# One hybrid decoder trunk on one core: the order in which the three mixers' pieces are traced

## The chip, the core and the metric

The kernel runs on 1 core of one Trainium2 chip. The time is microseconds of device time for one execution, from the first to the last instruction and what the launch adds around them. The engines are named as in the profile: PE (matmul) with PEld (its weight loads), DVE (vector), ACT (scalar), POOL, and SP, which here only issues DMAs.

## The reference

Two layers over 256 tokens of width 1024, batch 1, all float32. Each layer does:

```
h      = RMSNorm(x) * (1 + scale) + shift            # scale, shift, gate from silu(c) @ ada_w
cols   = h @ w_in                                    # 1024 x 9544
y_rw   = RWKV-7(cols)   # 8 heads of 64, delta-rule state, needs an inverse of a triangular matrix per 128 tokens
y_ssd  = Mamba-2 SSD(cols)  # conv of width 4, 4 groups x 4 heads, chunks of 128
y_fox  = FoX attention(cols)  # 8 heads of 64, causal, forget-gate bias
merged = sum_b sigmoid(gate_b) * (y_b @ proj_b)
x      = x + gate * (merged @ w_out)
x      = x + gate_f * FFN(h')    # layer 0: dense SwiGLU 2816; layer 1: top-2 of 8 experts of 3584
```

## The kernel before

Activations lie transposed in SBUF: features on 128 partitions, the 256 tokens in the free dimension. Every large product is done in three matmuls (`mm3`, line 124): a float32 weight is split into a high part (ACT, line 156) and a rest (DVE, line 157), and high x high, high x rest and rest x high are summed in PSUM. One **projection step** is 128 output columns over K = 1024: 24 matmuls of 256 columns, and two pairs of splits of 128x512. `stationary` (377) does two steps in one PSUM bank of tag `pd`; `project_rows` (391) does 256 columns into a `pd` and a `ps` bank; `project_cols` (386) loads the weight and calls `stationary`.

**The mixers of a layer** are Python generators. `rwkv_half` (487), called for two halves of 4 heads, r0 and r1, has the projections of k, r, v; then elementwise work on DVE and ACT, the pair matrices (line 612), a block inverse in six doubling levels (lines 649 to 674, with 32x32 transposes on DVE at 654), the state products (693 to 731) and the group norm (736 to 746). `ssd_group` (789), s0 to s3, has four projection steps with the convolution (799 to 805), the chunk products, and two gate projection steps (869). `fox_half` (898), f0 and f1, has three `project_rows` whose banks ACT copies out at line 906, then attention for four heads. `gates` (967) projects one branch's gate for all of `merged`; `merge` (976) multiplies one branch's y by its projection, for the other two branches with their gates, and adds.

**The order written out** is `ORDER` (51): a list for each layer of names, walked by lines 1376 to 1405. Each name runs its generator to its next `yield`, and there are few of these: r0 and r1 have four pieces (projections; all up to the pair matrices; all levels; state products, then the end), an s group three, an f half three, a merge one for each quarter. `mo` and `md` take the next half part of the modulation vectors of later sub-layers: 2 MB of `ada_w` are loaded (line 210; `mo`: four loads of 512 KB into two buffers `araw`; `md`: eight of 256 KB into buffers `u`), and eight operations of 128x512 on DVE (223, 225) sum them. The first merge is that of RWKV in the list before (`m0`), with its gates in `G`.

The instructions are not run in the order traced: line 1493 asks the framework to lay out each engine's queue by its own timing estimate, in which the trace order is the preference between those that are ready. The projections among themselves keep the trace order, as their weight loads do on SP's queue. What the pieces share: 3 weight buffers `raw` of 1 MB, 5 pairs `hi`/`lo`, 15 buffers `u` (all of RWKV's and FoX's values and the sums of `mo`), 4 buffers `b8` (y of RWKV and FoX, pair matrices, `merged`), 2 PSUM banks `pd`, 4 `pm`, 2 `ps`.

Of the kernel before, what the change touches and what calls it, by code (L numbers as in the profile page):

```python
# [63 lines left out]
def trunk(  # L64
# [312 lines left out]
    def stationary(raw, n, evac):  # L377

        ps = dbank()
        for q in range(0, n, P):  # L380
            m = min(P, n - q)
            o = ps[:m, q * 2:q * 2 + T]
            accumulate(o, raw[:, :, q:q + m], (hh, hl))
            evac(q // P, o)

    def project_cols(wsrc, c0, n, evac):
        for p0 in range(0, n, 256):
            w = min(256, n - p0)
            stationary(load_raw(rows(wsrc, 0, D, c0 + p0, w), KD, w), w, lambda i, ps: evac(p0 // P + i, ps))

    def project_rows(wsrc, c0, y):
# [3 lines left out]
        for kg in range(4):  # L395
            hi, lo = split_part(raw[:, 2 * kg:2 * kg + 2, :])
            for t in range(2):
                tb = slice(t * P, (t + 1) * P)
                for k in range(2):
                    kt = 2 * kg + k  # L400
                    mm3(ps[t], (y[0][:, kt, tb], y[1][:, kt, tb]), (hi[:, k, :], lo[:, k, :]), kt == 0, kt == KD - 1)
        return ps
# [33 lines left out]
    def stages(f):  # L436

        def start(*a):
            g = f(*a)
            return lambda: next(g, None)  # L440
        return start
# [17 lines left out]
    def rwkv(mx, l, prm, lora):  # L459
# [10 lines left out]
        project_cols(w_in[l], 1536, 288, lambda i, ps: shift(wa if i == 0 else gl[:ps.shape[0], i - 1, :], ps, 12 + i))  # L470
# [14 lines left out]
        return [y[:, 0], y[:, 1]], lambda jp: stages(rwkv_half)(mx, l, prm, lora, jp, shift, wa, gl, vd, vup, y)  # L485

    def rwkv_half(mx, l, prm, lora, jp, shift, wa, gl, vd, vup, y):
# [8 lines left out]
        for dst, g in ((k, 1), (r, 0), (v, 2)):  # L496
            project_cols(w_in[l], g * RW + jp * 256, 256, lambda i, ps: shift(dst[:, i, :], ps, 4 * g + 2 * jp + i))
# [14 lines left out]
        for jj in J:  # L512
            js = slice((2 * jp + jj) * P, (2 * jp + jj + 1) * P)
            for dst, hb, base in ((s, 0, W0), (th, 1, A0)):
                ps = mbank()[:, :T]
                mm(ps, wau[hblock(hb), js], wa[hblock(hb), :])
                act.activation(dst[:, jj, :], ps, AF.Tanh, scale=0.5, bias=col(pph, base, jj))
        dve.tensor_scalar_add(s, s, 1.0)
# [16 lines left out]


# [6 lines left out]
        for t in range(2):  # L543
            for jj in J:
                mm(ps[:, t * 4 + 2 * jj:t * 4 + 2 * jj + 2], sq[:, jj, t * P:(t + 1) * P], headsel)
        ss, rs = small(8, "r"), small(8, "r")
# [9 lines left out]


# [17 lines left out]


# [4 lines left out]


# [5 lines left out]
        act.activation(vrow, ps, AF.Copy)  # L588
        ps = mbank().rearrange("p (c f) -> p c f", c=2)
# [3 lines left out]
        act.activation(brow, ps, AF.Copy)  # L593

# [6 lines left out]
        for ch in range(2):  # L601
# [4 lines left out]
            for dst, src in ((mats[:, 0], bt), (mats[:, 1], kt)):  # L606
                for hb in range(2):
                    ps = mbank()
                    hp = hblock(hb)
                    for jj in J:  # L610
# [3 lines left out]
                                        ps.rearrange("p (q m) -> p q m", q=2))  # L614
            mbs.append(mats[:, 0])
            mks.append(mats[:, 1])
        yield
# [23 lines left out]
        for ch in range(2):  # L641
# [6 lines left out]
            act.activation(tls[ch], pz, AF.Copy)  # L648
        for lv in range(1, 6):
            odd = slice(1, 4, 2) if lv == 5 else slice(0, 4)  # L650
            for ch in range(2):
                pz = level(ch, lv, tls[ch])
                for q in range(4):
                    dve.transpose(blk(bds[ch], q)[:, odd, bcol(q)], by4(blk(pz, q))[:, odd, :])  # L654
            for ch in range(2):
# [10 lines left out]
            for ch in range(2):  # L666
# [5 lines left out]
                if lv == 4:  # L672
                    for n in range(4):
                        pool.tensor_copy(blk(tms[ch], n)[:, :, bcol(n)], by4(blk(tls[ch], n)))
        for ch in range(2):
# [4 lines left out]
            act.activation(ums[ch], pz, AF.Copy)  # L680
        h0, h1 = slice(0, 64), slice(64, 128)
# [10 lines left out]
        yield  # L692
        for ch in range(2):
# [10 lines left out]
            for hb in range(2):  # L704
                act.activation(halves(rr, hb), pb[hb][:, 0:2, :], AF.Copy)
            psa = mbank().rearrange("p (q f) -> p q f", f=64)
# [3 lines left out]
            act.activation(sa, psa[:, 0:4, :], AF.Copy)  # L710

# [10 lines left out]
            act.activation(yc, py, AF.Copy)  # L722
            pr = mbank()[:, :256]
# [8 lines left out]


# [13 lines left out]
        yield  # L747
# [750 lines left out]
```

## Time and profile before

| | |
|---|---|
| time, median of 3 runs | 2234.21 us (2226.03 to 2235.48) |
| the profiled execution | 2224.52 us |
| its span, first to last instruction | 2222.8 us |
| PE, PEld, DVE, ACT, POOL busy in it | 2115.0, 1811.2, 1798.8, 1386.1, 152.1 us |
| mean granted TensorE clock | 0.970 |

The page gives busy times; ends of matmuls in it are modelled, so a busy PE is not a PE at its full rate. Stages are read by cutting the span into stretches and asking busy time, number of instructions and granted clock (1.00 is 2.4 GHz, 0.50 is 1.2 GHz) of each. The stretches used: layer 0's first RWKV half from 60 to 182 us, its second half to 306, FoX and the merges to 478; then the output projection, the dense FFN and the next norm to 722; layer 1's RWKV halves from 750 to 876 and to 1026, its FoX and merges to 1168; the output projection and the experts to the end.

### The profile page before, as it was taken

The page shows a single profiled execution, that of the slowest core. Times are in us where ns is not written, and L with a number is a line of the kernel's source. Part 1 is how long each engine was busy: PE and PEld are TensorE (multiplying, and loading weights), DVE is VectorE, ACT ScalarE, POOL GpSimd, SP SyncE. Part 2 cuts the span into 40 slices and gives each one's busy share as a digit, 9 for nine tenths or more (in the row PEclk, how much of TensorE's full clock was granted, in tenths as well). Part 3 has the DMA queues.
Part 4 walks back from the last instruction along what each step waited for, and adds up shares of the span by engine and source line. Part 5 has one row for each costly group of instructions (what it writes and reads, how often), then busy time and mean ns, then how long its engine had stood idle before and what let it go on. Part 6 is the DMA issues. An engine that isn't in the chain of part 4 may idle for free.

```text
span 2222.8 us, 35724 instructions
## 1 busy us (share of the span) xinstructions
PE 2115.0 (95%) x13489; PEld 1811.2 (81%) x13489; DVE 1798.8 (81%) x2822; ACT 1386.1 (62%) x2204; POOL 152.1 (7%) x180
## 2 busy tenths in 40 slices
PE   7899899999998889989998999999999999999998
PEld 4777789998997877868998788888888887888776
DVE  4977776777776797756768999999999989999887
ACT  3454455555454545434555877878878777878775
POOL 2211200000000031211002000000000000000000
PEclk9999999999999998988998999999999999999999
DMA  8423254667884533414556999999999999999994
GB/s 304 128 83 95 77 172 156 213 198 259 294 286 137 145 108 93 138 53 130 184 176 251 337 362 359 324 368 367 374 337 352 355 362 336 342 364 368 336 363 151
DMA packets 316101, 546.68 MB, mean 246 GB/s; under 512 B 11952, under 2 KB 143536, under 8 KB 315920
## 3 DMA queue, kind: packets, MB, share of 16 engines
q1 hardware_dynamic: 315920, 544.31, 71.1%
q8 instruction: 108, 1.77, 0.3%
q14 instruction: 73, 0.60, 0.1%
HBM read 543.22 MB, written 1.05 MB: 245 GB/s over the span
## 4 chain that ended last, share of the span: by engine, by line
PE 79%; DVE 13%; issue 3%; ACT 2%; DMA 2%; POOL 0%; SPq 0%; DVEq 0%; ACTq 0%; POOLq 0%
PE pd L122 37%; PE pm L122 33%; PE ps L122 7%; DVE lo L157 5%; PE pm L131 1%; DVE u L654 1%; DMA araw<-in_ada_w_dram 1%; PE ps L131 1%; ACT hi L156 1%; DMA b<-in_ada_w_dram 1%; DVE cu L802 1%; DVE xr L1257 1%; DVE u L225 0%; DMA raw<-in_moe_w_gu_dram 0%; DVE b L612 0%
## 5 line engine op out<-in xcount | busy, mean ns | idle before, releaser
L156 ACT ACTIVATE hi<-raw 128x1024 fp32r<-128x1024 f32 (+2 forms) x1201 | 1027.7, 870 | 522.4 <-PE pd L122 277.0
L157 DVE TENSOR_TENSOR lo<-raw,hi 128x1024 fp32r<-128x1024 f32 (+2 forms) x1197 | 1154.6, 990 | 211.6 <-ACT hi L156 189.8
L122 PE MATMUL pd<-hh,hi 128*128 128x256 f32 (+2 forms) x1208 | 352.7, 293 | 15.3 <-ACT hh L362 3.9
L122 PE MATMUL pd<-hh,lo 128*128 128x256 f32 (+2 forms) x1208 | 346.5, 287 | 0.0
L122 PE MATMUL pd<-hl,hi 128*128 128x256 f32 (+2 forms) x1208 | 345.7, 286 | 0.3
L122 PE MATMUL pm<-lo,hh 128*128 128x512 f32 x672 | 266.7, 397 | 3.0 <-DVE lo L157 2.8
L122 PE MATMUL pm<-hi,hh 128*128 128x512 f32 x672 | 266.9, 397 | 0.1
L122 PE MATMUL pm<-hi,hl 128*128 128x512 f32 x672 | 263.0, 392 | 0.0
L122 PEld LDWEIGHTS pd<-hh,hi 128*128 128x128 f32 (+2 forms) x1208 | 231.9, 192 | 28.3 <-issue 5.6
L122 PEld LDWEIGHTS pd<-hh,lo 128*128 128x128 f32 (+2 forms) x1208 | 231.5, 192 | 6.1 <-issue 3.9
L122 PEld LDWEIGHTS pd<-hl,hi 128*128 128x128 f32 (+2 forms) x1208 | 232.7, 193 | 4.3 <-issue 2.3
L122 PE MATMUL pd<-lo,hi 128*128 128x512 f32 x448 | 174.7, 390 | 0.0
L122 PE MATMUL pd<-hi,hi 128*128 128x512 f32 x448 | 170.9, 391 | 0.1
L122 PE MATMUL pd<-hi,lo 128*128 128x512 f32 x448 | 167.8, 389 | 0.0
L122 PEld LDWEIGHTS pm<-lo,hh 128*128 128x128 f32 x672 | 126.8, 189 | 32.1 <-DVE lo L157 5.5
L122 PEld LDWEIGHTS pm<-hi,hh 128*128 128x128 f32 x672 | 126.5, 188 | 29.3 <-ACT hi L156 1.4
L122 PEld LDWEIGHTS pm<-hi,hl 128*128 128x128 f32 x672 | 126.7, 189 | 26.5
L122 PE MATMUL pm<-hi,more 128*128 128x512 f32 x448 | 142.1, 392 | 0.0
L122 PEld LDWEIGHTS pd<-hi,hi 128*128 128x128 f32 x448 | 84.1, 188 | 18.4 <-ACT hi L405 0.5
L122 PEld LDWEIGHTS pd<-hi,lo 128*128 128x128 f32 x448 | 84.1, 188 | 17.8
L122 PEld LDWEIGHTS pd<-lo,hi 128*128 128x128 f32 x448 | 84.1, 188 | 17.6
L122 PEld LDWEIGHTS pm<-hi,more 128*128 128x128 f32 x448 | 84.1, 188 | 17.5 <-ACT hi L156 0.3
(423 smaller groups left out, 3467.0 us busy)
## 6 DMA issues: line engine op xcount, KB each, us to landing
raw<-in_moe_w_gu_dram SPq DMA_DIRECT2D x224, 1024.0 KB, 7.0
raw<-in_moe_w_down_dram SPq DMA_DIRECT2D x110, 1024.0 KB, 6.8
raw<-in_w_in_dram SPq DMA_DIRECT2D x66, 1024.0 KB, 5.4
araw<-in_ada_w_dram SPq DMA_DIRECT2D x68, 512.0 KB, 4.3
raw<-in_ffn_w_gu_dram SPq DMA_DIRECT2D x22, 1024.0 KB, 6.8
raw<-in_ffn_w_down_dram SPq DMA_DIRECT2D x11, 1024.0 KB, 6.5
raw<-in_w_in_dram SPq DMA_DIRECT2D x16, 512.0 KB, 5.1
raw<-in_proj_ssd_dram SPq DMA_DIRECT2D x8, 1024.0 KB, 5.2
```

The costliest lines, as they stand in the source:

```text
L122: pe.matmul(o, lhsT, rhs, start=start, stop=stop)
L131: pe.transpose(o, i, ident[:n, :n])
L156: act.activation(hi, raw, AF.Copy)
L157: minus.tensor_sub(lo, raw, hi.bitcast(F32))
L654: dve.transpose(blk(bds[ch], q)[:, odd, bcol(q)], by4(blk(pz, q))[:, odd, :])
L802: dve.scalar_tensor_tensor(cu[:, s:T], ps[:, 0:T - s], pph[:, w:w + 1], cu[:, s:T], op0=ALU.mult, op1=ALU.add)
L1257: dve.tensor_add(xr[:, t, hs], xr[:, t, hs], po)
```

## The change

Every generator gets a `yield` after each projection step and each link of its chain of small operations: an RWKV half now has 45 steps, an s group 14, an f half 21, the gates 9, the first merge 9, the others 17 (`STEPS`). `ORDER` becomes one list of segments for both layers; a segment has one to three streams, and their steps are traced in turn, spread evenly over the segment. "`r1:25`" is 25 steps of r1, "`s2.`" what is left of s2. The gates made ahead are those of SSD (`b` = 1), which is merged first (`ma`), RWKV second (`mb`), FoX third (`mc`). `md` is gone: all six (layer 0) and five (layer 1) half parts of the modulation go by `mo`. What each operation computes is unchanged; `project_out` and `rwkv`'s first projection are still run whole (`whole`).

```diff
-ORDER = [
-    (
-        "rw r0 r0 mo r0 r0 fx sd s0 s0 s0 s1 s1 s1 r1 r1 r1 r0 s2 mo s2 s2 f0 r1 r1 s3 mo G f0 mo G s3 s3 G "
-        "f0 G m0 f1 m0 f1 m0 md md m1 md m0 m1 m1 md f1 md md md m1 m2 gm m2 md m2 m2"
-    ).split(),
-    (
-        "rw r0 r0 mo r0 sd s0 s0 r0 r0 s0 s1 mo s1 s1 s2 r1 r1 G r1 s2 fx r1 G s2 r1 G s3 s3 mo f0 f0 s3 G m0 "
-        "f0 m0 mo m0 m0 f1 md f1 m1 m1 md md md gm m1 md m1 f1 m2 m2 m2 md md md m2"
-    ).split(),
+STEPS = dict(r=45, s=14, f=21, G=9, ma=9, mb=17, mc=17)
+ORDER = 2 * [
+    [
+        ["rw"], ["r0:7"], ["sd"],
+        ["r0:25", "s0. s1:4", "mo"],
+        ["r0:8", "s1. s2:4", "mo"],
+        ["r0.", "r1:7 s2:2", "mo"],
+        ["r1:25", "s2. s3. G:4", "mo"],
+        ["r1:8", "G. ma:4", "mo"],
+        ["r1.", "fx f0:8 ma:2"],
+        ["f0.", "ma. f1:7", "mo mo"],
+        ["f1.", "mb:8", "mo mo"],
+        ["mb.", "mo"], ["gm"], ["mc."],
+    ],
 ]
...
             accumulate(o, raw[:, :, q:q + m], (hh, hl))
             evac(q // P, o)
+            yield
...
-            stationary(load_raw(rows(wsrc, 0, D, c0 + p0, w), KD, w), w, lambda i, ps: evac(p0 // P + i, ps))
+            yield from stationary(load_raw(rows(wsrc, 0, D, c0 + p0, w), KD, w), w, lambda i, ps, i0=p0 // P: evac(i0 + i, ps))
...
+            for segment in ORDER[l]:
+                streams = [steps(stream) for stream in segment]
+                for _, _, name in sorted(((i + 0.5) / len(x), k, name) for k, x in enumerate(streams) for i, name in enumerate(x)):
+                    assert take(name), (name, counts, taken)
```

## Rows read from the trace of the kernel before

**Rows 1.** The page's head: the span, and busy us (share) xinstructions by engine.

```profile
span 2222.8 us, 35724 instructions
...
PE 2115.0 (95%) x13489; PEld 1811.2 (81%) x13489; DVE 1798.8 (81%) x2822; ACT 1386.1 (62%) x2204; POOL 152.1 (7%) x180
```

**Rows 2.** Stretch, length, busy us (x) of PE, PEld, DVE, ACT, POOL; clock; DMA, GB/s.

```profile
60.00:182.00 122.00, 107.28 (x917) 91.94 (x916) 92.72 (x208) 56.48 (x138) 23.51 (x27) 0.92 0.32 95
182.00:306.00 124.00, 113.75 (x976) 95.84 (x974) 93.91 (x214) 60.45 (x139) 29.00 (x32) 0.96 0.38 113
306.00:440.00 134.00, 132.92 (x1128) 124.23 (x1126) 97.96 (x189) 76.17 (x175) 5.41 (x6) 1.00 0.58 185
440.00:478.00 38.00, 38.00 (x318) 36.72 (x317) 25.41 (x48) 21.88 (x40) 0.00 (x0) 1.00 0.58 181
...
750.00:876.00 126.00, 112.81 (x958) 94.58 (x956) 105.59 (x234) 64.85 (x160) 28.89 (x31) 0.94 0.35 101
876.00:1026.00 150.00, 133.64 (x1060) 112.26 (x1061) 104.07 (x223) 65.96 (x149) 27.84 (x31) 0.88 0.33 99
1026.00:1138.00 112.00, 112.00 (x939) 103.82 (x938) 74.85 (x144) 62.89 (x140) 5.18 (x5) 1.00 0.52 167
1138.00:1168.00 30.00, 30.00 (x267) 30.00 (x266) 20.22 (x38) 17.67 (x33) 0.00 (x0) 1.00 0.68 210
```

**Rows 3.** The same view, 1000 to 1010 us.

```profile
1000.00:1010.00 10.00, 9.26 (x35) 5.51 (x35) 1.68 (x6) 0.89 (x3) 1.01 (x1) 0.50 0.00 0
```

**Rows 4.** The same, only instructions on tile lo: PE, PEld, DVE, POOL.

```profile
60.00:182.00 122.00, 42.74 (x144) 29.50 (x144) 25.64 (x36) 0.00 (x0) 0.92 0.32 95
182.00:306.00 124.00, 48.87 (x168) 32.98 (x168) 28.96 (x42) 0.00 (x0) 0.96 0.38 113
306.00:440.00 134.00, 77.85 (x279) 52.33 (x280) 47.86 (x70) 0.00 (x0) 1.00 0.58 185
...
750.00:876.00 126.00, 43.41 (x149) 29.39 (x148) 28.57 (x39) 0.00 (x0) 0.94 0.35 101
876.00:1026.00 150.00, 55.76 (x188) 38.30 (x188) 32.67 (x47) 0.00 (x0) 0.88 0.33 99
1026.00:1138.00 112.00, 65.56 (x235) 43.95 (x236) 39.37 (x58) 0.00 (x0) 1.00 0.52 167
```

**Rows 5.** In order of time: start us, us, instruction [idle before <-releaser]; r1's state products.

```profile
992.11 0.88 PE L122 MATMUL pm<-b,u 128*64 128x128 f32 x12 [0.47 <-ACT u L710]
```

**Rows 6.** As rows 4, on tile lo, in stretches of 10 us.

```profile
240.00:250.00 10.00, 0.00 (x0) 0.00 (x0) 0.00 (x0) 0.00 (x0) 0.86 0.01 2
...
870.00:880.00 10.00, 0.00 (x0) 0.00 (x0) 0.00 (x0) 0.00 (x0) 0.76 0.22 67
...
990.00:1000.00 10.00, 0.17 (x1) 0.00 (x0) 0.69 (x1) 0.00 (x0) 0.90 0.15 51
1000.00:1010.00 10.00, 0.00 (x0) 0.00 (x0) 0.00 (x0) 0.00 (x0) 0.50 0.00 0
```

**Rows 7.** In order of time, ACT, layer 1.

```profile
1011.45 0.56 ACT L758 ACTIVATE u<-pm,pcol 128x256 f32<-128x256 f32 x1 [6.13 <-PE pm L131]
1011.91 0.37 ACT L906 ACTIVATE u<-pd 128x256 f32<-128x256 f32 x1
```

**Rows 8.** In order of time, DVE, layer 0.

```profile
100.10 0.73 DVE L612 COPY_PREDICATED b<-mmask,pm 128x512 f32<-128x512 uint8 x1
...
100.92 0.70 DVE L805 SCALAR_TENSOR_TENSOR xb<-zt,cu 128x256 f32<-128x256 f32 x1
...
106.66 0.68 DVE L157 TENSOR_TENSOR lo<-raw,hi 128x512 fp32r<-128x512 f32 x1
107.26 0.28 DVE L644 TENSOR_TENSOR c<-pm,icomp 128x128 f32<-128x128 f32 x1
```

**Rows 9.** Line 225, 60 to 306 us: xcount, ns min/median/max, first to last start.

```profile
L225 DVE SCALAR_TENSOR_TENSOR u<-araw,silc,u x14: 730/744/1653, 87.6 to 281.6; 128x512 f32<-128x512 f32 x14
```

**Rows 10.** SP's waits, 750 to 1026 us: waited for, us in total, times, longest.

```profile
SPq L210 <- DVE u L225: 63.9, 11, 23.1
```

More of the change, by code (lines that the diff above doesn't have):

```diff
@@ L434, in pair, with whole @@
         return keep(a, [P, KD, T], F32R), keep(b, [P, KD, T], F32R)
[L436 to L441, printed above, removed]
+    def whole(g):
+        while True:
+            try:
+                next(g)
+            except StopIteration as e:
+                return e.value
     def hblock(hb):
@@ L555, in rwkv_half @@
         dve.tensor_mul(kk, kk, ps)
+        yield
         kn = u()
@@ L809, in ssd_group @@
             nc.sync.dma_start(raw[:, :, q * P:(q + 1) * P], rows(w_in[l], 0, D, XBC_OFF + 1024 + 512 * q + g * P, P))
-        stationary(raw, 256, lambda i, ps: conv(2 + i, ps))
-        project_cols(w_in[l], XBC_OFF + g * 256, 256, conv)
-        yield
+        yield from stationary(raw, 256, lambda i, ps: conv(2 + i, ps))
+        yield from project_cols(w_in[l], XBC_OFF + g * 256, 256, conv)
         hc = lambda a, ch, n=4: a[:, ch * 16 + 4 * g:ch * 16 + 4 * g + n]
@@ L1374, in trunk, with part, take @@
             dtr = small_cols(l, mx)
-            run = {}
-            for step in ORDER[l]:
+            run, made, counts = {}, {}, {}
+            done = object()
+            def part(step):
                 i = int(step[1]) if step[1:] in tuple("0123") else 0
-                if step == "rw":
-                    y_rw, rw = rwkv(mx, l, prm, lora)
-                elif step == "sd":
-                    y_ssd, sd = ssd(mx, l, prm, dtr)
-                elif step == "fx":
-                    y_fox, fx = fox(mx, l, prm, dtr)
-                elif step == "mo":
-                    mod_next(mx, 0)
-                elif step == "md":
-                    mod_next(mx, MOD_LEFT[l], True)
-                elif step == "gm":
+                if step == "G":
+                    made["merged"] = mx("b8", [P, KD, T], bufs=NB8)
+                    return gates(mx, l, prm, 1, made["merged"])
+                if step[0] == "m":
+                    b = (1, 0, 2)["abc".index(step[1])]
+                    return merge(mx, l, prm, b, made["merged"], made["y"][b], (proj_rw, proj_ssd, proj_fox)[b][l], (4, 8, 4)[b], b == 1)
+                return made[step[0]](i)
+            def take(token):
+                if token == "rw":
+                    made.setdefault("y", {})[0], made["r"] = rwkv(mx, l, prm, lora)
+                elif token == "sd":
+                    made["y"][1], made["s"] = ssd(mx, l, prm, dtr)
+                elif token == "fx":
+                    made["y"][2], made["f"] = fox(mx, l, prm, dtr)
+                elif token == "mo":
+                    mod_next(mx, MOD_LEFT[l])
+                elif token == "gm":
                     while mod_late and mod_late[0][2] == 2:
@@ L1391, in trunk, with steps @@
                     gm = keep("vfirst", [P, 2, 512]) if l == 1 else mx("u2", [P, 2, 512])
[L1392 to L1405 removed]
+                    made["gm"] = [gm[:, 0], gm[:, 1]]
+                    mod_row(lambda: unit(mx, 4, P), l, 2, 0.5, made["gm"])
+                else:
+                    if token not in run:
+                        run[token] = part(token)
+                    if run[token] is None:
+                        return False
+                    counts[token] = counts.get(token, 0) + 1
+                    if next(run[token], done) is done:
+                        run[token] = None
+                return True
+            taken = {}
+            def steps(stream):
+                names = []
+                for word in stream.split():
+                    name, _, n = word.rstrip(".").partition(":")
+                    n = STEPS[name if name in STEPS else name[0]] - taken.get(name, 0) if word[-1] == "." else int(n or 1)
+                    taken[name] = taken.get(name, 0) + n
+                    names += [name] * n
+                return names
+            for segment in ORDER[l]:
+                streams = [steps(stream) for stream in segment]
+                for _, _, name in sorted(((i + 0.5) / len(x), k, name) for k, x in enumerate(streams) for i, name in enumerate(x)):
+                    assert take(name), (name, counts, taken)
+            assert not any(run.values()), [k for k in run if run[k]]
+            merged, gm = made["merged"], made["gm"]
             dump(f"merged{l}", merged)
```

68 lines of the change are left out of this document (41 added, 27 removed).

## The prediction

> **What bounds the kernel now.** I read the head of the page first: PE is busy 2115.0 of 2222.8 us, every other engine 81% or less [rows 1]. PE sets the pace, and the change adds and removes no matmul: it can win only where PE waits or runs slowly, in the two stretches with mixers, 60 to 478 and 750 to 1168 us. The other 1387 us keep their order.
>
> Next the stages [rows 2]. FoX and the merges (306 to 478, 1026 to 1168) are full: PE 132.92 of 134, 38.00 of 38, 112.00 of 112, 30.00 of 30, the clock at 1.00 (2.4 GHz). The RWKV stages are not: PE 107.28 of 122, 113.75 of 124, 112.81 of 126, 133.64 of 150, the clock at 0.92, 0.96, 0.94, 0.88.
>
> Busy time flatters these stages. From 1000 to 1010 us PE counts as busy for 9.26 us with 35 small matmuls, at clock 0.50 (1.2 GHz) [rows 3]. The Trainium skill ("Perfetto Trace Analysis", Identifying the Most-Contended Engine) says that matmul busy share is a poor measure of headroom and that the share of weight loads is a better one. The row agrees: 5.51 of those 10 us. By PE's busy time the four RWKV stages leave 522 - 467.5 = 54.5 us as the most to be won, by the weight loads 522 - 394.6 = 127 us; the sum below uses neither.
>
> I count instead. Projection matmuls come in threes, one of which reads `lo`. In the pure stretches 440 to 478 and 1138 to 1168 all matmuls are projections: (38 + 30) / (318 + 267) = 0.116 us each [rows 2]. So a stage's projections take 3 x its lo matmuls x 0.116, and the rest of its time is shared by its small matmuls [rows 2, 4]:
>
> - 60 to 182: 432 projections, 50.1 us; 71.9 us left for 485 small ones, 0.148 each
> - 182 to 306: 504, 58.5; 65.5 for 472, 0.139
> - 306 to 440: 837, 97.1; 36.9 for 291, 0.127
> - 750 to 876: 447, 51.9; 74.1 for 511, 0.145
> - 876 to 1026: 564, 65.4; 84.6 for 496, 0.171
> - 1026 to 1138: 705, 81.8; 30.2 for 234, 0.129
>
> In the full stages a small matmul costs 0.128 us. At that price the first halves lose 71.9 - 62.1 = 9.8 and 8.7 us, the second halves 5.1 and 21.1. RWKV's own can be cheaper: twelve of its state products take 0.88 us, 0.073 each [rows 5]. As the other end I take 0.10, midway (an estimate): 23 and 23, 18 and 35. **Second halves: 26 to 53 us lost, middle 40. First halves: 18 to 46, middle 32.**
>
> **Where it is lost.** A full PE holds 28 lo matmuls in 10 us (318 / 3 in 38 us [rows 2]); 240 to 250 holds 0, 870 to 880 holds 0, 990 to 1000 holds 1, 1000 to 1010 holds 0, the clock down to 0.50 in the last [rows 6]. The cause is the order. In layer 1's list f0 stands ahead of the last call of s3, the fourth G and `m0`. Its first projections are done by 990 and sit in both `pd` banks; ACT copies them out only at 1011.91, right behind r1's last step at 1011.45, before which it was idle for 6.13 us [rows 7]. No projection passes them, so r1's tail runs alone. In layer 0 f0 stands ahead of r1's levels, and 240 to 250 has no projection either.
>
> **The change, part by part.**
>
> The second half. r1's pair matrices and levels (25 steps) are traced with what is left of s2, s3 and four G steps, its state products (8) with five G and four `ma` steps, and f0 begins only with r1's last five. G and `ma` write `merged`, not `u`, so they wait for no buffer of r1's. The hole of 990 to 1010 gets 5 x 24 matmuls of G and 4 x 24 of `ma`, 25 us for 20. I take three quarters of the 40 us, because two projections of f0 still meet r1's last five steps in both `pd` banks: -30 us. Ends: 0 and -53.
>
> The first half. r0 is woven with s0 and s1 already: DVE does s0's convolution (line 805) between r0's pair matrices and its first level [rows 8], although the list has all of r0 first. The trace order is only a preference. What is late there is DVE, 92.72 and 105.59 us busy of 122 and 126 [rows 2], and the change takes nothing off it. I take 0; ends +10 and -46, the loss above.
>
> The modulation sums. Before, two half parts fall in layer 0's RWKV stages: 14 operations of line 225 at 744 ns [rows 9], seven to a part. The new list has five of the six ahead of f0's chain; in layer 1 it has five `mo` there where three stood. A part is about eight operations, 8 x 0.744 = 6 us of DVE: 18 and 12 us more on a DVE that is 186.6 us busy of 246 in layer 0's RWKV stages (76%) [rows 2]. Where DVE is idle this costs nothing, where it delays a chain it costs all. I take a quarter, as DVE is full only in places: +8; ends 0 and +30. Their loads come with them: `mo` has two buffers `araw`, so the third load of a part waits on SP's queue for line 225 (63.9 us in 11 waits, the longest 23.1 [rows 10]), and the weight loads traced behind it wait too. Three `raw` buffers of 48 x 0.116 = 5.6 us of PE each cover the mean wait, 5.8 us, not the longest; the upper end has room for one such.
>
> SSD merged first instead of RWKV: the same 8 x 24 and 8 x 12 matmuls in another order, 0; what it allows is in the first item. The yields issue no instruction. `md` gone: its eight loads went where DVE had room; 0, covered by FoX's stage (DVE 97.96 of 134 [rows 2]).
>
> What is late next: FoX's stage shortens by what was moved into the holes, one for one, as long as FoX's chain does not set its end. Before, 38 and 30 us of pure merge lie behind that chain [rows 2]; after, the 17 `mc` steps do (8 x 24 + 8 x 12 = 288 matmuls, 33 us). So 15 us a layer fit.
>
> **Sum.** -30 + 0 + 8 = -22 us against the profiled execution's 2224.5 us (span 2222.8). That one is the fastest of the four executions shown, 9.7 us below the median of the three runs; the median of all four is 2230.1, and I take the 22 us from that: 2208.
>
> **The rivals.**
>
> Slower: the weave takes preference from the chains. r0, r1, f0 and f1 follow one another in each layer, 2 x 38 + 2 x 15 = 106 chain steps, and before, chain steps were traced ahead of the projections that filled their gaps. Now projections stand between them. If every step waits for one more split on DVE (0.68 us [rows 8]), the chains are 72 us longer a layer. 38 and 30 us of pure merge take up the first of it, so the change loses from about half the steps on. At two thirds: 48 - 34 = 14 a layer, 2258. For it: DVE at 76 to 84% in the first halves. Against: queues follow readiness more than the trace [rows 8]. Chance 0.23, 2246 to 2300.
>
> No change: the holes come from buffers. r1, f0 and the sums still share the 15 `u`, the projections two `pd` banks; the stall moves to another step, the 30 us shrink to about 10 and the sums eat 8: 2228. The Trainium skill ("Perfetto Trace Analysis", Optimization Strategy) says that consistent bubbles can mean too little SBUF or PSUM for the next tile; no buffer is added here. Against: G and `ma` need no `u`. Chance 0.20, 2221 to 2240.
>
> Larger gain: the weave also feeds PE in the first halves and holds the clock at 1.00: half of the 32 besides 40, the sums free, -56: 2174. Chance 0.13, 2150 to 2190. The forecast, 2190 to 2221, has 0.44.
>
> **Numbers.** A measurement tells about 0.5%, 11 us, from no change; around 2234.2 that is 2223 and 2245. Faster: 0.13 + 0.44 = 0.57; same 0.20; slower 0.23. The range cuts the far halves of the large gain and of the slow case: 2172 to 2256.
>
> **What would show it.** Right: no 10 us between r1's levels and FoX's first copies (line 906) without lo matmuls; clock at 0.95 or more there; layer 1's mixers shorter by more than layer 0's. Right for the sums: DVE above 80% in the RWKV stages. Wrong: RWKV's chain (line 612 to line 746) longer than before while PE is full (the slow rival); the same holes at other steps (no change); PE full and shorter in the first halves too (the larger gain).

## The result, and the profile after

The changed kernel takes 2253.62 us, the median of four executions (2250.86 to 2256.42). The kernel before, beside it, takes 2231.12 us (2226.03 to 2235.48, four). The ratio is 1.0101, with an interval of [1.0077, 1.0126]: slower by 1.0%. The prediction had 2208 us; 2253.62 lies inside its range of 2172 to 2256, but on the other side of no change.

The head of the page after (span; busy us and instructions of each engine), to be held against [rows 1]:

```profile
span 2249.1 us, 35650 instructions
...
PE 2135.5 (95%) x13489; PEld 1834.0 (82%) x13489; DVE 1792.2 (80%) x2822; ACT 1384.2 (62%) x2204; POOL 155.6 (7%) x180
```

The same 13489 matmuls keep PE busy 20.5 us longer than in [rows 1]. No work came in for PE: it ran slower, at a mean granted clock of 0.960 instead of 0.970, and waited more.

The stages. The columns are those of [rows 2]; each layer is cut at the first tanh of r0, the first tanh of r1, the last group norm of r1 and where FoX's chain ends (the pure merges that follow take 38 and 32 us, as before 38 and 30). Layer 0, then layer 1:

```profile
62.00:223.00 161.00, 145.56 (x1175) 127.65 (x1174) 124.53 (x273) 77.51 (x185) 28.37 (x31) 0.89 0.42 125
223.00:374.00 151.00, 135.85 (x1141) 117.93 (x1139) 103.75 (x223) 67.85 (x151) 29.70 (x31) 0.92 0.40 122
374.00:462.00 88.00, 86.33 (x705) 77.93 (x704) 56.89 (x114) 48.82 (x116) 5.07 (x6) 0.99 0.45 139
...
772.00:920.00 148.00, 134.56 (x1089) 116.05 (x1087) 121.21 (x270) 74.26 (x181) 29.64 (x31) 0.91 0.41 120
920.00:1074.00 154.00, 138.25 (x1154) 120.36 (x1152) 106.54 (x228) 68.15 (x151) 29.74 (x31) 0.91 0.39 120
1074.00:1164.00 90.00, 88.06 (x716) 78.98 (x716) 52.67 (x102) 50.48 (x119) 4.45 (x4) 1.00 0.39 118
```

By the same marks the kernel before has 60, 183, 301 and 440 us, and 750, 893, 1010 and 1138 ([rows 2] cuts a little later). So the two RWKV stages of layer 0 grew from 241 to 312 us and those of layer 1 from 260 to 302. FoX's stages became shorter, 139 to 88 and 128 to 90, because more of the projections was done by then, but not by as much. The granted clock in the four RWKV stages is 0.89, 0.92, 0.91 and 0.91; by the same marks it was 0.92, 0.96, 0.92 and 0.91.

The prediction's own count shows where the 26 us went. The matmuls on tile `lo` in the same stretches, as in [rows 4]:

```profile
62.00:223.00 161.00, 65.44 (x218) 46.17 (x218) 36.55 (x53) 0.00 (x0) 0.89 0.42 125
223.00:374.00 151.00, 61.26 (x211) 41.12 (x210) 36.76 (x53) 0.00 (x0) 0.92 0.40 122
374.00:462.00 88.00, 46.38 (x164) 30.88 (x164) 28.56 (x42) 0.00 (x0) 0.99 0.45 139
...
772.00:920.00 148.00, 56.73 (x189) 39.38 (x188) 32.27 (x47) 0.00 (x0) 0.91 0.41 120
920.00:1074.00 154.00, 61.97 (x214) 42.24 (x214) 38.20 (x55) 0.00 (x0) 0.91 0.39 120
1074.00:1164.00 90.00, 47.10 (x170) 31.83 (x170) 28.84 (x42) 0.00 (x0) 1.00 0.39 118
```

Three times these at 0.116 us, the rest of the stretch for its small matmuls, 0.128 us for each of them as the price of a full PE, and what is left is lost. For the first row: 161 - 654 x 0.116 = 85.1 us, less 521 x 0.128 = 66.7, leaves 18.4. In the order of the rows 18.4, 12.5, 3.7, 15.4, 14.0 and 4.5 us are lost, 68.5 in all. Before it was 9.8, 5.1, 0, 8.7, 21.1 and 0, 44.7 in all, with the stretches of [rows 2 to 4]. The difference of 23.8 us is nearly all of the 26.3 us between the spans. In this list the second half of layer 1, from which most of the gain was expected, seems to lose less than before, 14.0 us for 21.1; but [rows 2] counts the 16 us behind r1's last norm to it. With the kernel before cut by the same marks as the changed one, its list is 10.6, 4.3, 0, 14.5, 11.4 and 4.1 us, with nearly the same sum, and every stage loses more after. The second half of layer 1 by these marks, all instructions and those on `lo`:

```profile
893.00:1010.00 117.00, 105.23 (x863) 86.04 (x861) 74.56 (x172) 48.73 (x114) 23.07 (x28) 0.91 0.28 81
...
893.00:1010.00 117.00, 39.08 (x135) 26.31 (x134) 24.62 (x35) 0.00 (x0) 0.91 0.28 81
```

### The profile page after: what moved, and what is told of

Read it like the earlier page. It is cut to its first block, busy times and chain, and to the rows that moved or that the text cites. A ratio compares the mean times of both kernels' runs of the same rounds, so it can differ in the third digit from the quotient of the medians.

```text
span 2249.1 us, 35650 instructions
## 1 busy us (share of the span) xinstructions
PE 2135.5 (95%) x13489; PEld 1834.0 (82%) x13489; DVE 1792.2 (80%) x2822; ACT 1384.2 (62%) x2204; POOL 155.6 (7%) x180
## 4 chain that ended last, share of the span: by engine, by line
PE 77%; DVE 14%; DMA 3%; issue 3%; ACT 2%; POOL 0%; SPq 0%; DVEq 0%; ACTq 0%; POOLq 0%
PE pd L129 37%; PE pm L129 30%; PE ps L129 7%; DVE lo L164 6%; DMA araw<-in_ada_w_dram 2%; PE pm L138 2%; PE ps L138 1%; DVE cu L829 1%; ACT hi L163 1%; DVE u L232 1%; DVE u L674 1%; DMA xr<-in_x_dram 1%; DVE xr L1291 1%; DVE b L631 0%; DMA raw<-in_moe_w_gu_dram 0%
## 5 line engine op out<-in xcount | busy, mean ns | idle before, releaser
L129 PE MATMUL pd<-hh,hi 128*128 128x256 f32 (+2 forms) x1208 | 360.0, 300 | 21.8 <-DVE cu L829 11.0
L129 PE MATMUL pd<-hl,hi 128*128 128x256 f32 (+2 forms) x1208 | 353.5, 293 | 0.1
L129 PE MATMUL pd<-hh,lo 128*128 128x256 f32 (+2 forms) x1208 | 352.1, 292 | 0.9 <-DVE lo L164 0.9
L129 PEld LDWEIGHTS pd<-hh,hi 128*128 128x128 f32 (+2 forms) x1208 | 238.6, 198 | 38.8 <-issue 13.9
L129 PEld LDWEIGHTS pd<-hl,hi 128*128 128x128 f32 (+2 forms) x1208 | 239.3, 198 | 5.6 <-issue 3.8
L129 PEld LDWEIGHTS pd<-hh,lo 128*128 128x128 f32 (+2 forms) x1208 | 238.4, 198 | 6.2 <-issue 3.3
L129 PEld LDWEIGHTS pd<-hi,hi 128*128 128x128 f32 x448 | 84.3, 188 | 18.4 <-ACT hi L415 0.3
```

What stands on the lines that cost most here:

```text
L129: pe.matmul(o, lhsT, rhs, start=start, stop=stop)
```

## Where the time went: the chain's links wait behind whole projections

I followed RWKV's chain through each half by the start times of its operations: from the first tanh (line 528, 517 before) over the last pair matrix (631, 612 before), the six levels, the copies of the state products (728, 734, 747; 705, 710, 722 before) to the last group norm (773, 746 before). Summed over the four halves of the two layers it takes 484 us before and 605 after. Of the 120 us between them (all rounded), 29 lie ahead of the last pair matrix, 36 from there to the first product of the first chunk, 11 between the chunks, and 45 in the tail, from the second chunk's first product to the last norm (57 us before, 102 after).

The tail of layer 0's r0 is the plainest: 17 us before, 37 after. Here is ACT in that stretch of the changed kernel, in order of time (start us, us, instruction, idle before and what ended it). Line 728 is the second chunk's first product; its next link is the copy of line 734:

```profile
182.08 0.43 ACT L728 ACTIVATE u<-pm 128x128 f32<-128x128 f32 x2
182.40 0.57 ACT L826 ACTIVATE cu<-pd,pph 128x256 f32<-128x256 f32 x1
187.03 0.81 ACT L831 ACTIVATE zt<-cu 128x256 f32<-128x256 f32 x2 [4.07 <-DVE cu L829]
188.15 0.63 ACT L415 ACTIVATE ysh<-s 128x512 fp32r<-128x512 f32 x1 [0.30 <-DVE s L914]
189.75 0.63 ACT L163 ACTIVATE hi<-raw 128x512 fp32r<-128x512 f32 x1 [0.97 <-PE pd L129]
192.45 0.63 ACT L163 ACTIVATE hi<-raw 128x512 fp32r<-128x512 f32 x1 [2.08 <-PE pd L129]
193.81 0.63 ACT L163 ACTIVATE hi<-raw 128x512 fp32r<-128x512 f32 x1 [0.73 <-PE pd L129]
194.35 0.55 ACT L826 ACTIVATE cu<-pd,pph 128x256 f32<-128x256 f32 x1
194.80 0.62 ACT L163 ACTIVATE hi<-raw 128x512 fp32r<-128x512 f32 x1
195.32 0.46 ACT L478 ACTIVATE u<-pd,omu 128x256 f32<-128x256 f32 x1
195.67 0.38 ACT L734 ACTIVATE u<-pm 128x256 f32<-128x256 f32 x1
```

And PE's small matmuls around it:

```profile
184.23 1.54 PE L129 MATMUL pm<-u,u 128*128 128x64 f32 x6
...
196.11 0.66 PE L129 MATMUL pm<-b,u 128*64 128x128 f32 x8 [0.88 <-ACT u L734]
```

The last matmuls of that form ahead of the copy end at 185.77. The copy starts at 195.67, 9.9 us later, although ACT is idle for 5.3 of them: ahead of it in the queue stand a tanh that waits for the convolution on DVE, three weight splits that wait until PE's projections give back a `hi` buffer, and a copy of a projection's bank. PE then waits 0.88 us for that copy itself. From start to start the link takes 13.6 us. The Trainium skill ("PSUM — Partial Sum Buffer", Engine vs sequencer instructions) says that the queues of ScalarE and VectorE are strictly first in, first out. The trace agrees: the copy's matmuls were done 9.9 us before it started. In the kernel before, the same link takes 4.1 us from start to start:

```profile
168.19 0.54 ACT L705 ACTIVATE u<-pm 128x128 f32<-128x128 f32 x2
172.28 0.39 ACT L710 ACTIVATE u<-pm 128x256 f32<-128x256 f32 x1 [2.51 <-PE pm L122]
```

What stands between the links is seen in the chain of waits of the changed kernel (start us, us, what):

```profile
176.79 6.21 DMA araw<-in_ada_w_dram
...
183.11 0.75 DVE u L232
...
187.00 7.36 PE pd L129 x47
...
195.78 0.28 ACT u L734
...
197.50 5.85 PE pd L129 x48
...
210.75 7.27 PE pd L129 x48
```

A projection step is 24 matmuls, so the last three are two whole steps each time, 20.5 us in three runs, about the 20 us by which this tail grew (a run of one step, 2.74 us, lies between the second and the third). The new list says so: in `["r0.", "r1:7 s2:2", "mo"]` the last five steps of r0 are spread over nine others, and in `["r1.", "fx f0:8 ma:2"]` those of r1 over ten. In the kernel before, the chain of waits has runs of 1, 10 and 13 projection matmuls in that tail, and one of 30 from 183.51 us, just ahead of the last norm.

Ahead of the first run of the changed kernel the chain goes through a part of the modulation sums: DVE is idle for 1.1 us until its load has landed, and the convolution that the tanh on ACT waits for stands behind it. So the sums have a share in this link, though a small one beside the projections.

The hole of [rows 6] did not go either. Four of the stretches of 10 us with the fewest matmuls on `lo` after (columns as in [rows 4]):

```profile
240.00:250.00 10.00, 2.09 (x7) 1.33 (x7) 2.08 (x3) 0.00 (x0) 0.94 0.34 105
250.00:260.00 10.00, 2.06 (x5) 1.65 (x5) 0.69 (x1) 0.00 (x0) 0.55 0.01 2
...
350.00:360.00 10.00, 0.00 (x0) 0.09 (x1) 0.10 (x1) 0.00 (x0) 0.56 0.55 189
...
1050.00:1060.00 10.00, 0.26 (x1) 0.34 (x1) 0.00 (x0) 0.00 (x0) 0.54 0.23 78
```

The last two lie in r1's last steps. G and the first four steps of `ma`, which were to fill them, had run ahead: layer 0's r1 copies its first product only at 339 us, and the fourth output of the first merge was written at 333.

What holds the other projections there is f0, as the prediction read it in the kernel before. Here is the hole of layer 0 (PE's projections before and after it, ACT's copies between them; line 935 copies f0's banks out, as 906 did before):

```profile
346.98 0.28 PE L129 MATMUL ps<-hi,hl 128*128 128x256 f32 x1
...
357.02 0.38 ACT L734 ACTIVATE u<-pm 128x256 f32<-128x256 f32 x1 [3.33 <-PE pm L129]
357.30 0.38 ACT L935 ACTIVATE u<-pd 128x256 f32<-128x256 f32 x1
...
359.75 0.58 PE L129 MATMUL pd<-hi,hh 128*128 128x256 f32 x1
```

f0's second projection is done at 347.3. Its banks' copies stand on ACT behind r1's copies, and no projection runs for 12.5 us; in layer 1 it is 12.3 us, from 1047.1 to 1059.4. So the waiting goes both ways: links of the chain wait behind projections, and projections' banks behind links.

## The experiments

Three theories stood against each other. Preference: woven projections go ahead of RWKV's chain, and its stages wait for it. Sums: the modulation parts that were moved into these stages delay it. Buffers: the holes come from banks and buffers that are held too long. All ratios are to the kernel before on the same chip, from three rounds.

### The chain's steps ahead of the woven ones

Within a segment all steps of r0 or r1 are traced first, then the others in their order:

```diff
-for _, _, name in sorted(((i + 0.5) / len(x), k, name) ...
+for _, _, name in sorted(((i + 0.5) / len(x) - (k == 0 and name[0] == "r"), k, name) ...
```

> The changed kernel with one edit: in each segment all RWKV steps are traced before the steps woven with them. Three theories of the 1.0% loss. Preference (the trace of the changed kernel: layer 0's RWKV stages take 312 us from r0's first tanh to r1's last norm, 241 before): projections traced between the chain's steps go ahead of them in PE's and DVE's queues; then both RWKV halves fall back to about 250 us a layer, the time to at most that of the kernel before (ratio 0.985 to 1.000). Sums (three more parts of modulation on DVE in the RWKV stages): nothing of that changes here, ratio 1.005 to 1.012. Buffers (f0's banks behind r1's tail): the holes at r1's tail stay, ratio 1.005 to 1.012.

Measured: 2212.18 us, 0.9924 [0.9896, 0.9952]; the chain 526 us, its tail 69. One edit in the order of the trace takes 1.8% off the changed kernel and makes it faster than the kernel before. The RWKV stages fall back to 273 and 279 us a layer, for 312 and 302, and not to the 250 that Preference expected. No sum leaves its segment and no buffer is added, but each sum is now traced behind its segment's RWKV steps, so this run alone does not part Preference from Sums; the runs with the sums late, below, do.

### The chain's steps behind the woven ones

The same with `+ (k == 0 and name[0] == "r" and len(streams) > 1)`.

> The changed kernel with the opposite edit of chain_first: in each segment the RWKV steps are traced after all the steps woven with them. Preference: the chain is later still, ratio to the kernel before 1.02 to 1.05, and layer 0's time from r0's first tanh to r1's last norm above the changed kernel's 312 us. If only the evenness of the weave mattered (bursts instead of a spread), chain_last would gain as chain_first did, ratio below 1.00.

Measured: 2264.77 us, 1.0155 [1.0136, 1.0174], slower as Preference says, but by less than its 1.02; the chain 643 us, its tail 133. The first half's stage in this kernel, layer 0, is 173 us long, for 161 in the changed one:

```profile
61.00:234.00 173.00, 156.49 (x1250) 138.96 (x1247) 133.49 (x290) 82.94 (x194) 25.30 (x29) 0.88 0.42 125
```

The chain goes by its place in the trace, in both directions.

### Only the tails ahead

The first edit for the segments "r0." and "r1." alone (`- (segment[0] in ("r0.", "r1.")) * (k == 0)`).

> The changed kernel with one edit: only the last five steps of r0 and of r1 are traced before the projections woven with them (segments r0. and r1.). Preference: r0's second chunk takes 37 us from its first copy to its last norm in the changed kernel and 17 before, r1's 21 and 15; about 20 us of layer 0's RWKV time and as much of layer 1's come back, ratio 0.995 to 1.003. If preference matters in the long weave of pair matrices and levels instead: ratio 1.008 to 1.012. Sums: no change, 1.010.

Measured: 2239.87 us, 1.0054 [1.0035, 1.0074]. The ratio lies between what was expected of the tails and of the long weave. The tail goes from 102 to 55 us, about that of the kernel before (57), and the preparation stays (189 to 183). So the nine and ten steps woven into these five are what made the tail long, and the tails are about a quarter of what the first edit gained in time.

### The modulation sums later

Three of five `mo` moved from the RWKV segments to those of f0, f1 and `mb`:

```diff
-        ["r0:8", "s1. s2:4", "mo"],
-        ["r0.", "r1:7 s2:2", "mo"],
+        ["r0:8", "s1. s2:4"],
+        ["r0.", "r1:7 s2:2"],
...
-        ["r1:8", "G. ma:4", "mo"],
+        ["r1:8", "G. ma:4"],
```

> The changed kernel with three of the five modulation parts in the RWKV stages of each layer moved into FoX's segments. Sums: 12 to 18 us of DVE a layer leave the RWKV stages, time 10 to 25 us shorter, ratio 0.998 to 1.006. Preference and buffers: at most 5 us, ratio 1.007 to 1.011.

Measured: 2236.18 us, 1.0034 [1.002, 1.0048]; the chain 579 us. That looks like 0.7% for the sums, though the two holes of 12 us at r1's end are gone here too. But with the chain's steps first as well they are worth nothing:

> chain_first and mo_late together. If the two costs are separate (0.018 and 0.007 of the time of the kernel before): ratio 0.983 to 0.989. If with the chain traced first the sums fall into idle time of DVE (in chain_first two of the five parts already run after r0's levels): ratio 0.989 to 0.994.

Measured: 2217.57 us, 0.9946 [0.9927, 0.9965], against 0.9924 with the sums where they were. The two together don't show a cost of the sums; and the even weave with its steps shifted, below, comes out 0.6 and 0.8% under the changed kernel without moving a sum out of its segment.

### The merge kept for r1's tail

`ma` taken from r1's products and put ahead of f0 in r1's last five steps:

```diff
-        ["r1:8", "G. ma:4", "mo"],
-        ["r1.", "fx f0:8 ma:2"],
+        ["r1:8", "G.", "mo"],
+        ["r1.", "ma:6 fx f0:8"],
```

> The changed kernel with the SSD merge's first six steps moved from r1's state products and from behind f0 to r1's last five steps, ahead of f0. Buffers: 350 to 360 us holds no projection in the changed kernel (1 matmul), as 1000 to 1010 before; six merge steps of 24 matmuls (17 us) now lie there, about 10 us a layer shorter, ratio 0.998 to 1.004. Preference: merge steps woven into r1's tail hold it up as the f0 projections did, ratio 1.006 to 1.014.

Measured: 2240.93 us, 1.0062 [1.004, 1.0084], 13 us under the changed kernel. That lies in Preference's range and just above that of Buffers. The hole of layer 1 is gone in it, that of layer 0 goes from 12.5 to 6.8 us, and the chain is 21 us shorter too, so the run does not tell which of them gave the time. The same on top of the chain first and the late sums:

> first_late with the SSD merge's first six steps behind r1's last steps and ahead of f0. If f0's banks still hold up projections at r1's tail: 4 to 10 us shorter than first_late. If r1's tail is covered by now: within 3 us of first_late.

Measured: 2228.39 us, 0.9987 [0.9972, 1.0001], worse than the 0.9946 without it. No projection waits longer than 5 us at r1's end in this kernel, where first_late, the one without the edit, has 7.5 us in layer 1. Holding fill back for the hole closes it, and gains nothing once the chain is short.

### The kernel before with f0 behind r1

This was meant to test the prediction's reading of the hole [rows 6, 7]: in the old list f0 is traced after r1's tail, so that its projections would not sit in both `pd` banks.

```diff
-s2 mo s2 s2 f0 r1 r1 s3 mo G f0 mo G s3 s3 G f0 G m0
+s2 mo s2 s2 r1 r1 s3 mo G mo G s3 s3 G f0 f0 f0 G m0
...
-s3 s3 mo f0 f0 s3 G m0 f0 m0
+s3 s3 mo s3 G f0 f0 m0 f0 m0
```

> The kernel before with one edit to its list: f0's first pieces traced after r1's tail, and in layer 1 the last s3 piece and the last gates ahead of f0. This tests how the prediction read the holes of the kernel before, 990 to 1010 us above all. If f0's results in both pd banks are what holds the other projections: the hole fills, 8 to 20 us shorter, ratio 0.991 to 0.997. If the chain's own latency with nothing else ready makes the hole: ratio 0.998 to 1.006.

Measured: 2247.85 us, 1.0079 [1.0052, 1.0106], above both ranges. In layer 0 the edit does what it was made for: f0's first copy comes at 323 us, behind r1's last norm at 305 (269 and 301 before). There r1 keeps its length (118 us before, 121 here), no more projections run beside it, and FoX's stage grows from 139 to 154 us (305 to 459; by the same marks it ran from 301 to 440). The row of that stage, and a stretch in it on tile `lo`:

```profile
305.00:459.00 154.00, 142.44 (x1143) 131.48 (x1143) 99.74 (x187) 76.31 (x168) 9.63 (x8) 0.94 0.52 168
...
365.00:375.00 10.00, 0.00 (x0) 0.00 (x0) 0.00 (x0) 0.00 (x0) 0.84 0.05 18
```

FoX's stage, full in [rows 2], now has a hole of its own. In layer 1 the edit does not do what it was made for: f0's first projections still run ahead of the end of r1's tail. The last projection matmul, f0's first copy (for the kernel before in [rows 7]) and the next projection, first in the kernel before, then here:

```profile
990.01 0.28 PE L122 MATMUL ps<-hi,hl 128*128 128x256 f32 x1
...
1012.41 0.56 PE L122 MATMUL pd<-hi,hh 128*128 128x256 f32 x1
...
1020.49 0.28 PE L122 MATMUL ps<-hi,hl 128*128 128x256 f32 x1
...
1037.33 0.37 ACT L906 ACTIVATE u<-pd 128x256 f32<-128x256 f32 x1
...
1037.82 0.56 PE L122 MATMUL pd<-hi,hh 128*128 128x256 f32 x1
```

Both times the next projection begins half a microsecond after f0's first copy. The same is true in layer 1 of nine more of the kernels here, with holes of 6 to 22 us. So the reading of the hole in layer 1 stands, and this run does not test it there. What a hole costs is another question. Layer 1's second half takes 166 matmuls on `lo` here, 135 before, and that brought no time; nor did closing the hole in the kernel of the section before this one.

### FoX's steps ahead as well

The first edit with `name[0] in "rf"`.

> chain_first with FoX's steps too traced ahead of what is woven with them in the two segments of f0 and f1. Preference holds a chain dear only where its stage waits for it: in chain_first the stage from r1's last norm to FoX's last projection of a head takes 101 us a layer with PE full, and 36 us of pure merge lie behind it, so FoX's chain is covered: ratio 0.989 to 0.996, the same as chain_first (0.9924). A rival, that any chain gains by being traced first whatever lies behind it, would take some of FoX's two stages as r0 and r1 gave 0.018: 0.985 or less.

Measured: 2223.91 us, 0.9969 [0.9952, 0.9987]: just outside the range of Preference, and not better than r0 and r1 alone (0.9924; the intervals touch). The rival that any chain gains by being traced first is out.

### Half the lead

The steps of r0 and r1 at half their spacing, `(i + 0.5) / len(x) / (1 + (k == 0 and name[0] == "r"))`.

> The changed kernel with the RWKV steps at half their spacing in each segment: they run through the first half of it, the woven steps stay where they were. Preference, if it goes by the number of projection steps that stand ahead of a chain step: half of them are gone, so half way between 1.0101 and 0.9924, ratio 0.998 to 1.004. If a small lead is enough: 0.992 to 0.995. If only standing wholly ahead helps: 1.007 to 1.011. Sums and Buffers by themselves expect the changed kernel's 1.0101, since neither a sum nor a buffer is taken away.

Measured: 2203.2 us, 0.9873 [0.9843, 0.9902], the fastest of all, and below all that was expected. The stage of its second half in layer 1:

```profile
885.00:1019.00 134.00, 127.96 (x1132) 112.39 (x1132) 109.23 (x233) 68.50 (x158) 25.50 (x29) 0.99 0.45 142
```

This is what the prediction wanted: 1132 matmuls in 134 us at a clock of 0.99, where [rows 2] has 1060 in 150 at 0.88 (cut by the same marks, the kernel before has 863 in 117 us at 0.91). But half the lead gaining more than all of it is not what Preference by itself says, so two more doses were run, factors of 0.75 and 0.25 on the spacing.

> The changed kernel with the RWKV steps at three quarters of their spacing: half the lead of chain_half. Preference as the runs so far give it (last 1.0155, even 1.0101, half spacing 0.9873, wholly first 0.9924) is a smooth curve with its least between half spacing and wholly first: 0.994 to 1.002 here. If the framework's order flips with every small shift of the trace, so that 0.9873 was one lucky draw, the value lies off the curve: above 1.005 or below 0.987.

> The same at a quarter of their spacing: between half spacing (0.9873) and wholly first (0.9924). A smooth curve gives 0.985 to 0.993; a lucky draw at half spacing gives 0.992 to 0.998 here, chain_first's neighbourhood.

Measured: 2228.26 us, 0.9972 [0.9948, 0.9996], and 2228.71 us, 0.9991 [0.9976, 1.0007]. The first is where a smooth curve wants it; the second lies above all that was expected of it. With a lead of any size the ratio lies between 0.9873 and 0.9991, without a rule in the size of the lead.

### The order of the merges

First the control: the chain first, and all of `ma` after r1 (`["r1:8", "G.", "mo"], ["r1.", "fx f0:8"]`).

> chain_first with the four steps of ma moved out of r1's state products and the two out of its last five, into f0's segment: the control for the next kernel. What SSD merged first allows, fill for r1's tail, is gone: if that fill carries chain_first's gain, the ratio goes from 0.9924 to 0.997 to 1.000 (the nearest run, with ma ahead of f0 and the sums late, gave 0.9987); if it carries none, 0.991 to 0.995.

Measured: 2214.08 us, 0.9919 [0.9893, 0.9946], as with `ma` in r1's tail. Then the same with RWKV merged first and SSD second:

```diff
-                    return gates(mx, l, prm, 1, made["merged"])
+                    return gates(mx, l, prm, 0, made["merged"])
...
-                    b = (1, 0, 2)["abc".index(step[1])]
+                    b = (0, 1, 2)["abc".index(step[1])]
```

> The control before it with RWKV merged first and SSD second, as in the kernel before; no step of another stream moves. The prediction held that the order of the branches by itself is worth 0: within 0.003 of the control. If keeping SSD's y longer or freeing RWKV's y sooner matters, it differs by 0.005 or more (10 us), either way.

Measured: 2220.73 us, 0.9949 [0.993, 0.9969]. The order of the branches is worth 0.3%, with intervals that overlap: little or nothing.

### How much of it is a draw

Every step of the changed kernel a quarter of a spacing earlier, `(i + 0.25) / len(x)`, and later, `(i + 0.75) / len(x)`. The weave stays as even as it was; single steps change places with a neighbour of another stream, and the sum of a segment moves.

> The changed kernel with every step's place in its segment a quarter of a spacing earlier: the weave is as even as before, single steps change places and the sum of a segment moves from its middle to its first quarter. If the even weave is slow by itself, as Preference holds, 1.003 to 1.014. If the changed kernel's 1.0101 was an unlucky draw, it falls among the kernels with a lead: 0.987 to 0.999.

> The same a quarter of a spacing later. Preference: 1.003 to 1.014. An unlucky draw: 0.987 to 0.999.

Measured: 2234.62 us, 1.0018 [1.0009, 1.0028], and 2239.65 us, 1.0039 [1.0027, 1.0051]. The chains take 583 and 596 us, so the even weave makes them long each time, but the loss is 0.2 and 0.4% where the changed kernel has 1.0. The second lies in the range of Preference, the first below it and above that of the unlucky draw. Then the kernel before with one sum a place later in each layer (`r0 mo r0` to `r0 r0 mo`; `mo G` to `G mo` and `mo f0` to `f0 mo`):

> The kernel before with the first part of the modulation sums one piece of r0 later in both layers. If the order flips with small shifts, before is a draw as well, and this lies up to 0.006 from it on either side; if its order is steady, 0.997 to 1.003.

> The kernel before with one sum of each layer a place later, behind a G step in layer 0 and behind f0's first piece in layer 1. As for the one before it: 0.997 to 1.003 if the order is steady, up to 0.006 away if before is a draw like the others.

Measured: 2232.88 us, 1.0022 [1.0008, 1.0037], and 2225.03 us, 0.9978 [0.9965, 0.9992]. Both lie in the range of a steady order, though each interval leaves out 1: a change that should mean nothing moves this kernel by 0.2%. The three even weaves lie 0.2 to 0.8% apart.

### All of them together

The chain is the sum of the four halves, preparation up to the last pair matrix, tail from the second chunk's first product; each is worked out from start times in that kernel's timeline. The span is that of the profiled execution, which can differ from the median: for "even weave, later" it is the slowest of ten, 2250.14 us for a median of 2239.65.

| kernel | preparation | tail | chain, us | span, us | ratio |
|---|---|---|---|---|---|
| before | 160 | 57 | 484 | 2222.8 | 1 |
| before, one sum later | 160 | 52 | 487 | 2227.2 | 1.0022 |
| before, another sum later | 160 | 57 | 485 | 2221.7 | 0.9978 |
| before, f0 behind r1 | 160 | 56 | 493 | 2247.5 | 1.0079 |
| chain first, `ma` after r1 | 165 | 60 | 510 | 2212.2 | 0.9919 |
| the same, RWKV merged first | 164 | 61 | 510 | 2218.9 | 0.9949 |
| chain first, sums late | 155 | 68 | 513 | 2215.0 | 0.9946 |
| the same, `ma` ahead of f0 | 165 | 68 | 523 | 2230.5 | 0.9987 |
| r and FoX first | 165 | 70 | 525 | 2228.8 | 0.9969 |
| chain first | 166 | 69 | 526 | 2209.5 | 0.9924 |
| half spacing | 174 | 81 | 540 | 2201.9 | 0.9873 |
| quarter spacing | 184 | 68 | 544 | 2224.0 | 0.9991 |
| tails first | 183 | 55 | 552 | 2233.6 | 1.0054 |
| three quarters of the spacing | 169 | 75 | 567 | 2226.2 | 0.9972 |
| sums late | 186 | 100 | 579 | 2234.3 | 1.0034 |
| even weave, earlier | 182 | 95 | 583 | 2233.1 | 1.0018 |
| `ma` ahead of f0 | 190 | 82 | 584 | 2238.7 | 1.0062 |
| even weave, later | 179 | 95 | 596 | 2248.4 | 1.0039 |
| the changed kernel | 189 | 102 | 605 | 2249.1 | 1.0101 |
| chain last | 234 | 133 | 643 | 2272.0 | 1.0155 |

Among the sixteen kernels with small steps, span and chain go together: a straight line through them has 0.38 us of span for each us of chain, a correlation of 0.86, and leaves 9 us of scatter. The first edit changed nothing but the place of RWKV's steps in the trace, and chain and span both fell. But the line holds between the groups and not within the first of them: among the nine kernels with a lead the correlation is 0.19, with chains of 510 to 567 us and spans of 2201.9 to 2230.5. The chain's length tells an even weave from a lead; it does not tell which lead is fast. The kernels of the old list don't lie on that line: their chain is the shortest of all, but FoX's stages are long (139 and 128 us in the kernel before, 101 and 101 with the chain first, 88 and 90 in the changed one). That is how a lead can win over the kernel before although its chain is longer.

The nine kernels in which r0's and r1's steps lead in every segment lie between 0.9873 and 0.9991; the six with an even weave, or with the tails alone ahead, between 1.0018 and 1.0101. That the even weave is slower than one with a lead is shown. That it is 1.0% slower than the kernel before is true of this one kernel; of its three draws the mean is 1.0053, and why this draw is worse than the other two is open. So is why half spacing is the best by half a per cent: neither its chain nor its tail is the shortest, and its neighbours at a quarter and three quarters gain 0.1 and 0.3%.

## Why the prediction was wrong, point by point

- **What bounds the kernel.** Right in part. The time is in the RWKV stages and the count by projections and small matmuls closes on the difference of the spans (23.8 of 26.3 us). But the count says how much PE loses, not to whom. The loss was read as missing work for PE, to be had by putting work there. Work woven in evenly made the chain longer, by 120 us over the four halves, and that was put at nothing. PE's busy share is 95% before and after.
- **The second half, -30.** Wrong, and the step by which the sum failed. By the prediction's own cuts [rows 2, 4] the two second halves lost 26.2 us before, by the marks used here 15.7; after the change they lose 26.5. So the 30 us came out as a loss of 0 to 11. The chain, for which the term had nothing, grew from 118 and 117 us to 151 and 154. The steps that were to fill the hole ran ahead, and the hole came back at 347 and 1047 us. The cause given for it, f0 in both `pd` banks [rows 7], is right for layer 1, and the prediction kept a quarter of the loss for it. What failed is the step from the loss to a gain: the work went ahead of the hole and not into it, and it held up the chain that the hole belongs to.
- **The first half, 0.** Wrong by less, for the same reason: the halves lose 18.4 and 15.4 us, by the same marks 10.6 and 14.5 before, and the chain takes 157 and 143 us for 125 and 124. "The trace order is only a preference" rested on one convolution between two levels [rows 8]. The framework does reorder, but the tail read above shows that a link on ACT waits for what is queued ahead of it, and that a preference is enough to put 47 projection matmuls there.
- **The sums, +8.** Not shown. DVE is busy 77, 69, 82 and 69% in the four stages, not above 80 throughout, and SP waited for them 47.8 us in 13 waits, the longest 12.5 (772 to 1074 us), where [rows 10] has 63.9 in 11 and 23.1. Moved away they gave 0.7% once and nothing the other time. The one delay of the chain by them that is read here is the 1.1 us of DVE in the tail above.
- **SSD first, 0.** Held within the measurement: 0.3%. What it allows, `ma` in r1's tail, is worth nothing either: 0.9919 without it, 0.9924 with it.
- **The rival "slower"** was the one that came. Its price was near: at two thirds of the steps it had 48 us a layer and 2258 us, the chains grew by 60 a layer and the time is 2253.62. Its place was not. It had every link wait 0.68 us on DVE; what was found, in the tail read above, is a link that waits 9.9 us on ACT and runs of two whole projection steps on PE between links; the tails, where the list weaves two steps to each, took 45 of the 120 us. Nor was it only the pure merges that took up the first of it: FoX's stages gave back 51 and 38 us, as they had less left to do. The sign it named, the chain longer while PE is full, was half right; PE is busy 90% there.
- **"No change"** was right that holes come back at other steps, and that f0's `pd` banks are behind those at r1's end. That they set the time was not shown: the merge kept for r1's tail closed these holes or made them smaller, and one kernel was 13 us faster by it and another 11 us slower.
- **The chances.** 0.23 for this rival and 0.57 for faster were the wrong way round. The new list gave a warning that was not read: five steps spread over nine and over ten in the two tails.

## What to carry to other kernels

When throughput work is woven with a chain of short dependent steps, weave it with a lead: trace the chain's steps ahead of the steps woven with them, and count for each segment how many long steps fall to one link. Nine kernels with a lead of some kind took 0.9873 to 0.9991, and none of them shows which lead is best. The Trainium skill ("Perfetto Trace Analysis", Optimization Strategy) says that interleaving regimes with different busiest engines may improve performance; here the same interleave gave 1.0018 to 1.0101 even and 0.9873 to 0.9991 with a lead, so the order inside it decides. And where a framework lays out the queues, shift an order a little in two or three ways before its ratio is believed to half a per cent.

## What the runs showed of the hardware

Here a hole was paid for twice. The 47 projection matmuls that begin at 187.00 us start at the lower of the two clock levels. The columns are those of [rows 2]:

```profile
187.00:190.50 3.50, 3.50 (x16) 3.50 (x17) 2.81 (x8) 2.07 (x4) 0.26 (x1) 0.50 0.41 144
191.00:194.30 3.30, 3.30 (x32) 3.30 (x30) 0.79 (x2) 1.12 (x2) 0.00 (x0) 1.00 0.64 165
```

At 0.50 (1.2 GHz), after a stretch of small matmuls and short waits, 16 take 3.5 us, 0.22 each; at 1.00 (2.4 GHz) 32 take 3.3 us, 0.10 each. The 16 cost 1.8 us more than at full clock, and the link behind them waits for that too.
